# Projection weights: halves split for the first token half kept in DRAM and fetched for the second; gate differences on VectorE

## The chip, the cores and the metric

The kernel runs on one core of a Trainium2 chip. The metric is device time in microseconds, from the launch of the program to its end. The engines are named as in the profile: PE is TensorE's matmul, PEld its weight load, DVE is VectorE, ACT ScalarE, POOL GpSimd, and SP SyncE, which here only issues DMAs. A name such as SPq or POOLq is the engine's instruction queue.

## The reference

One layer over 1024 tokens of 1024 channels, all in float32: a norm with a shift and a scale that depend on the conditioning vector `c`, a wide input projection, two mixers (a pooling mixer and a gated linear attention), an output projection with a gated residual, then a second norm and a gated MLP with a causal convolution.

```python
mod = c_act @ ada_w[l] + ada_b[l]
sh1, sc1, g1, sh2, sc2, g2 = jnp.split(mod, 6, axis=-1)
h = modulate(rmsnorm(x), sh1, sc1)
u, q, k, v, r, z = jnp.split(h @ w_in[l], IN_SPLITS, axis=-1)
y_pool = pool_mixer(u, w_pool[l], pool_scale[l])
y_gla = gla_mixer(q, k, v, r, z, w_gate2[l], b_gate[l], gla_norm[l])
y = jnp.concatenate([y_pool, y_gla], axis=-1) @ w_out[l]
x = x + g1[:, None, :] * y
h = modulate(rmsnorm(x), sh2, sc2)
x = x + g2[:, None, :] * conv_ffn(h, w_up[l], conv_w[l], conv_b[l], w_down[l])
...
return rmsnorm(x) * final_norm
```

In the attention, `b` is the running sum of log gates; a score of two tokens carries `exp` of a difference of two such sums.

## The kernel before

Channels lie on the 128 partitions, in 8 tiles; the 1024 tokens are two halves of 512. Every projection is computed for the first half and later again for the second, with the same weights, since only then are the second half's activations there.

**Split products.** A float32 product is made of three faster ones. A weight tile of 512 KB is loaded into one of four buffers (`raw`, from the pool `rawp`, L62), ACT casts it to its high part `wh` (L152), DVE subtracts that from it, which gives the low part `wl` (L153), and `mm3` (L113) multiplies high by high, high by low and low by high. Two buffers each hold `wh` and `wl`. The four raw buffers also serve the tiles `ada` of the conditioning product (L215 to L220: a load by SP, then a DVE product whose sum goes into `modv`), of which 20 come beside the projections r, u and out. `load_w` (L156) does load and split; it runs for each tile in each half.

**Jobs.** A job is one weight tile's work: `job_proj` (L612) 24 matmuls for one output tile of q, k, r or u, `jobs_v` (L636) and `jobs_out` (L667) two channel tiles of four outputs. `run_jobs` (L726) calls the load of the next job, runs the present one, then issues its `ada` products. In the second half the groups are k, z, q, k, v, q, then r0 to r3, then u0 to u3 (L761 to L763); `jobs_out(0)` follows, the output projection of the first half, then `jobs_out(1)`.

**Order.** PE's order is written out by the program: beside the jobs run generators (attention, pooling, norms) that are resumed when a counter of estimated PE time passes their due time. The order of the other engines is made by a scheduler from dependences; each engine then runs its own in order, SP's queue of DMA issues too.

**The attention** (`gla_pair`, L382) goes through seven levels for each of two pairs of heads in each half. For a level `gla_prep` (L337) takes a difference of gate sums `le` (POOL, L343 or L347), ACT takes exponentials (L351, L352), DVE makes `kl` (L356) and `lq` (L359), PE multiplies them (`sc`), and DVE copies the scores under a mask into `la` (L376). POOL makes `kd` (L403) and `le<-k,lb`, the product of q and k for the diagonal `dg` (L390).

**The ends.** The pooling mixer `pool_tail` (L511) copies u out of PSUM on ACT (`us`, L515), makes sums on DVE (L522), a difference (L532) and its split `dh`, `dl`, and a small product `po`, whose result goes to `yh` (ACT, L540) and `yl` (DVE, L541). The output projection adds to x on DVE and stores x1 to DRAM by SP (L695); the squares of x1 are added up on POOL (`nsa`, L234) for the second norm.

Of the kernel before, what the change touches and what calls it, by code (L numbers as in the profile page):

```python
# [28 lines left out]
P = 128  # L29
NK = 8  # L30
# [23 lines left out]
def trunk_kernel(ctx, tc, xT, cvec, adaT, vecs, w_start, w_z, w_qkru, w_v, w_g2, w_pool,  # L54
# [98 lines left out]
        dve.tensor_tensor(out=wl, in0=raw, in1=wh.bitcast(F32), op=ALU.subtract)  # L153
        return wh, wl

    def load_w(dram, shape=(P, NK, P)):  # L156
        raw = raw4(shape=shape)
        nc.sync.dma_start(out=raw, in_=dram)
        return split_w(raw, shape)

    def split_a(src, name):
        h, l = s2(F32R, name=name + "h"), s2(F32R, name=name + "l")
# [174 lines left out]
    def gla_prep(b, k, q2, h):  # L337
        nb = T // (2 * h)
        bb = blocks(b, h)
        e = tmp("le")  # L340
        eb = blocks(e, h)
        if h == 1:
            pool_e.tensor_tensor(out=eb[:, :, 1], in0=bb[:, :, 1], in1=bb[:, :, 0],  # L343
                                 op=ALU.subtract)
            kl = k
        else:
            pool_e.tensor_tensor(out=e.rearrange("p (n h) -> p n h", n=nb),  # L347
                                 in0=b.rearrange("p (n h) -> p n h", n=nb),
                                 in1=bb[:, :, 0, h - 1:h].broadcast_to([P, nb, 2 * h]),
                                 op=ALU.subtract)  # L350
            act.activation(out=eb[:, :, 0], in_=eb[:, :, 0], func=AF.Exp, scale=-1.0 / 16)  # L351
        act.activation(out=eb[:, :, 1], in_=eb[:, :, 1], func=AF.Exp, scale=1.0 / 16)  # L352
        if h > 1:
            kl = klb[mark.setdefault("kl", 0)]
            mark["kl"] ^= 1
            dve.tensor_tensor(out=blocks(kl, h)[:, :, 0], in0=blocks(k, h)[:, :, 0],  # L356
                              in1=eb[:, :, 0], op=ALU.mult)
        ql = tmp("lq", shape=(P, 2, T // 2))
        dve.tensor_tensor(  # L359
            out=ql.rearrange("p e (n h) -> p e n h", h=h),  # L360
            in0=q2.rearrange("p e (n two h) -> p e n two h", two=2, h=h)[:, :, :, 1],
            in1=eb[:, :, 1].unsqueeze(1).broadcast_to([P, 2, nb, h]), op=ALU.mult)
        return kl, ql
# [18 lines left out]
    def gla_pair(hf, ct):  # L382
# [17 lines left out]
        for i, h in enumerate(LEVELS):  # L400
            nxt = gla_prep(b, k, q2, LEVELS[i + 1]) if i + 1 < len(LEVELS) else None
            if i == 0:
                pool_e.tensor_tensor(out=chunks(kd), in0=chunks(b),  # L403
                                     in1=chunks(b)[:, :, P - 1:P].broadcast_to([P, 4, P]),
                                     op=ALU.subtract)
                act.activation(out=kd, in_=kd, func=AF.Exp, scale=-1.0 / 16)
                dve.tensor_tensor(out=kd, in0=kd, in1=k, op=ALU.mult)
            gla_scores(av, *pre, h)
            if i == 3:
                ktp = stile("ktp", (P, 4, P))  # L410
                for c in range(4):
# [12 lines left out]
            if i == 6:
                for hd in range(2):
                    dve.tensor_tensor(out=q2[:, hd], in0=q2[:, hd], in1=eq, op=ALU.mult)
            yield LEVEL_STEP[hf]
# [181 lines left out]
        if t is not None:  # L609
            mod_tile(t, True)  # L610

    def job_proj(dram, hf, then, last=False):  # L612
        def run(w):
            wh, wl = w
            pp = ptile()
            for k in range(NK):
                until(lambda: hs[hf][k] is not None)
                mm3(pp, wh[:, k], wl[:, k], *hs[hf][k], k == 0, k == NK - 1)
                if last:
                    nacc["gone"] = k + 1  # L620
                if k < NK - 1:
                    tick()
            then(pp)
        return (lambda: load_w(dram)), run

    def job_z(hf):
        def run(_):
# [8 lines left out]
    def jobs_v(hf):  # L636
        pv = []

        def mk(kp):
            def run(w):  # L640
                wh, wl = w
                if kp == 0:
                    pv.extend(ptile() for _ in range(4))
                for j in range(2):
                    k = 2 * kp + j
                    h, l = hs[hf][k]
                    for c in range(4):
                        cs = slice(c * P, c * P + P)
                        mm(pv[c], h[:, cs], wh[:, j], k == 0, False)
                        mm(pv[c], l[:, cs], wh[:, j], False, False)  # L650
                        mm(pv[c], h[:, cs], wl[:, j], False, k == NK - 1)
                        tick()
                if kp == 3:
                    for c in range(4):
                        vt[hf * 4 + c] = s2(name="v")
                        act.copy(out=vt[hf * 4 + c], in_=pv[c])
            return (lambda: load_w(w_v[kp], (P, 2, T))), run
        return [mk(kp) for kp in range(4)]

    def job_u(hf, gi):  # L660
        return job_proj(w_qkru[8 + gi], hf, lambda pp: spawn(pool_tail(hf, gi, pp)),
                        hf == 0 and gi == 3)

    def job_r(hf, n):
        return job_proj(w_qkru[4 + n], hf, lambda pp: put_r(pp, hf, n))

    def jobs_out(hf):  # L667
        po = []

        def mk(i):  # L670
            d0, kp = 4 * (i // 4), i % 4

            def run(w):
# [7 lines left out]
                for j in range(2):  # L681
                    k = 2 * kp + j
                    until(lambda: ys[hf][k] is not None)
                    for n in range(4):
# [2 lines left out]
                        if k == NK - 1:  # L687
                            evac(d0 + n, po[n])
                        tick()
            return (lambda: load_w(w_out[i], (P, 2, T))), run  # L690

        def evac(d, pp):
            dve.scalar_tensor_tensor(out=x1[hf][d], in0=pp, scalar=modv[:, 16 + d:17 + d],  # L693
                                     in1=x1[hf][d], op0=ALU.mult, op1=ALU.add)
            nc.sync.dma_start(out=x1d[hf][d], in_=x1[hf][d])  # L695
            own = s2 if hf else None
            if d == 0:
                nacc[hf] = s2(name="nsa") if hf else tmp("nsa")
# [24 lines left out]
            hs[0][k] = mod_split(x1[0][k], 24, k)  # L723
            yield 2.0

    def run_jobs(jobs, mods_each=0):  # L726
        loaded = jobs[0][0]()
        for i, (_, run) in enumerate(jobs):
            nxt = jobs[i + 1][0]() if i + 1 < len(jobs) else None
            run(loaded)  # L730
            loaded = nxt
            for _ in range(mods_each):
                mod_next()
            tick()
# [6 lines left out]
    run_jobs([job_u(0, n) for n in range(4)])  # L741

    def job_q(ct):
        load, run = job_proj(w_qkru[ct], 1, lambda pp: put_q(pp, 1, ct))

        def go(w):
            until(lambda: ys[0][4 + 2 * ct] is not None)
# [1 line left out]
        return load, go  # L749

    def job_k(ct):
        return job_proj(w_qkru[2 + ct], 1, lambda pp: put_k(pp, 1, ct))

    named = {"z": job_z(1)}
    for ct in range(2):
# [4 lines left out]
        named[f"v{n}"] = j  # L760
    for names, mods_each in (("k0 z q0 k1 v0 v1 v2 v3 q1", 0), ("r0 r1 r2 r3", 2),  # L761
                             ("u0 u1 u2 u3", 1)):
        run_jobs([named[i] for i in names.split()], mods_each)  # L763
    run_jobs(jobs_out(0), 2)
    spawn(norm2_first())
    late = jobs_out(1)
    run_jobs(late[:5], 1)
    until(lambda: hs[0][7] is not None)
    ph1.close()
    phr.close()  # L770
# [507 lines left out]
```

## Time and profile before

| | us |
|---|---|
| median of 3 runs | 1082.6 |
| range of the runs | 1080.9 to 1084.25 |
| profiled execution | 1082.63 |
| its span | 1080.9 |
| PE busy | 1021.6 |
| DVE busy | 856.0 |
| ACT busy | 546.2 |
| POOL busy | 200.1 |

The span is the time from the first to the last instruction of the profiled execution. In all, DMA moved 152.64 MB. By stage: up to about 54 us the first half's norm and its k, q and two r tiles; to 189 us the rest of the first half's projections and its attention; to 337 us the second half's projections with its attention, then the first half's output; to 400 us the second half's output; behind that the MLP, which the change does not touch.

In a row of the timeline stand start, duration, engine, line, operation, output and inputs; in brackets how long the engine was idle before it, and what ended that. In a row of the waits stand the total in microseconds, the number of waits and the longest.

### The profile page before, as it was taken

The numbers are of one execution on the slowest core, as the hardware profiler recorded it, in microseconds if no ns is written. First come the engines' busy times: TensorE is split into PE (matmuls) and PEld (weight loads), VectorE is DVE, ScalarE is ACT, GpSimd is POOL, SyncE is SP. The second block draws the span as 40 slices with busy tenths as digits, with TensorE's granted clock in tenths as the row PEclk, the third lists the DMA queues.
The fourth block names the chain that finished last, engine by engine and source line by source line (L and its number), as shares of the span: only waits on it lengthen the run. The fifth ranks groups of instructions, "written<-read, shape, count | busy, mean of one in ns | idle before, by whom it ended". The sixth has DMA issues, their size and how long they took to land.

```text
span 1080.9 us, 12664 instructions
## 1 busy us (share of the span) xinstructions
PE 1021.6 (95%) x4480; PEld 816.2 (76%) x4480; DVE 856.0 (79%) x1189; ACT 546.2 (51%) x881; POOL 200.1 (19%) x171
## 2 busy tenths in 40 slices
PE   6989999999898986899999999999999999999986
PEld 4668878887786764688888888888888888888875
DVE  7967999688897959997776777767767686988884
ACT  5475484534534435655554555545545544644542
POOL 3436203131132115011011010010110100200210
PEclk8999999999899998999999999999999999999998
DMA  8743331454577530232223223322233895323542
GB/s 311 256 137 106 98 112 64 148 184 136 166 262 253 202 129 20 78 117 98 88 89 117 88 98 108 108 107 98 106 127 111 294 328 193 98 98 98 187 154 78
DMA packets 60385, 152.64 MB, mean 141 GB/s; under 512 B 6593, under 2 KB 9761, under 8 KB 60322
## 3 DMA queue, kind: packets, MB, share of 16 engines
q1 hardware_dynamic: 53760, 132.43, 36.2%
q0 software_dynamic: 4928, 17.30, 4.1%
q10 hardware_dynamic: 1634, 2.10, 0.6%
q8 instruction: 35, 0.57, 0.2%
q14 instruction: 28, 0.23, 0.1%
HBM read 126.12 MB, written 25.69 MB: 140 GB/s over the span
## 4 chain that ended last, share of the span: by engine, by line
PE 74%; DVE 16%; DMA 3%; ACT 3%; issue 3%; POOL 1%; SPq 0%; POOLq 0%; ACTq 0%; DVEq 0%
PE dn L107 18%; PE upy L107 17%; PE pp L107 14%; PE upz L107 11%; PE upx L107 10%; DVE wl L153 2%; PE sc L107 1%; DVE ada L219 1%; DVE hl L275 1%; DMA ada<-in_adaT_dram 1%; PE ss L107 1%; DVE la L376 1%; DMA da<-in_w_down_dram 1%; DVE sl L887 1%; DVE x L267 1%
## 5 line engine op out<-in xcount | busy, mean ns | idle before, releaser
L107 PE MATMUL dn<-ws,xs 128*128 128x512 f32 (+1 forms) x936 | 212.9, 389 | 2.8 <-DVE xs L1087 2.8
L107 PEld LDWEIGHTS dn<-ws,xs 128*128 128x128 f32 x936 | 175.3, 189 | 40.0 <-issue 3.7
L107 PE MATMUL upy<-sh,xs 128*128 128x512 f32 x272 | 92.2, 400 | 6.1 <-ACT upy L937 6.1
L107 PE MATMUL upy<-sh,ws 128*128 128x512 f32 x256 | 85.7, 395 | 0.9 <-ACT upy L937 0.9
L975 POOL DMA_DIRECT2D gd<-y x22 | 12.0, 545 | 372.6 <-DVE y L974 372.6
L793 DVE TENSOR_TENSOR xs<-ua,xs 128x512 fp32r<-128x512 f32 x77 | 54.8, 711 | 31.4 <-ACT xs L792 31.4
L153 DVE TENSOR_TENSOR wl<-raw,wh 128x1024 fp32r<-128x1024 f32 (+1 forms) x50 | 63.5, 1270 | 17.2 <-ACT wh L152 17.0
L107 PE MATMUL pp<-hl,wh 128*128 128x512 f32 x176 | 70.9, 403 | 5.4 <-DVE hl L275 5.4
L107 PE MATMUL pp<-hh,wh 128*128 128x512 f32 x176 | 73.9, 420 | 1.0 <-ACT hh L274 1.0
L792 ACT CAST xs<-ua 128x512 fp32r<-128x512 f32 x77 | 47.9, 622 | 52.1 <-PE upy L107 21.4
L107 PE MATMUL pp<-hh,wl 128*128 128x512 f32 x176 | 70.8, 402 | 2.3 <-DVE wl L153 2.3
L793 DVE TENSOR_TENSOR ws<-ua,ws 128x512 fp32r<-128x512 f32 x77 | 54.2, 704 | 22.1 <-ACT ws L792 22.1
L792 ACT CAST ws<-ua 128x512 fp32r<-128x512 f32 x77 | 48.0, 623 | 42.1 <-PE upy L107 20.6
L792 ACT CAST ws<-da 128x512 fp32r<-128x512 f32 x58 | 36.1, 622 | 63.9 <-PE dn L107 47.7
L107 PEld LDWEIGHTS upy<-sh,xs 128*128 128x128 f32 x272 | 51.8, 190 | 19.5 <-ACT upy L937 6.8
L803 DVE TENSOR_TENSOR ua<-ua 128x512 f32<-128x512 f32 x88 | 62.7, 713 | 2.2
L107 PE MATMUL upz<-sh,ws 128*128 128x512 f32 x184 | 62.2, 397 | 1.7 <-ACT sh L886 1.7
L152 ACT CAST wh<-raw 128x1024 fp32r<-128x1024 f32 (+1 forms) x50 | 50.4, 1008 | 24.1 <-PE pp L107 7.8
L107 PE MATMUL pp<-yh,wh 128*128 128x512 f32 x128 | 55.5, 434 | 6.7 <-ACT us L515 3.5
L107 PE MATMUL upx<-hh,xs 128*128 128x512 f32 x176 | 59.1, 397 | 2.4 <-ACT sp L953 2.4
L107 PE MATMUL upx<-hh,ws 128*128 128x512 f32 x176 | 59.3, 398 | 0.2 <-DVE x L693 0.2
L347 POOL TENSOR_TENSOR le<-b 128x512 f32<-128x512 f32 x24 | 33.7, 1406 | 137.7 <-PE dg L107 52.4
(252 smaller groups left out, 2461.1 us busy)
## 6 DMA issues: line engine op xcount, KB each, us to landing
ua<-in_w_up_dram SPq DMA_DIRECT2D x46, 512.0 KB, 3.3
ada<-in_adaT_dram SPq DMA_DIRECT2D x32, 512.0 KB, 3.8
gd<-y POOLq DMA_DIRECT2D x22, 512.0 KB, 2.9
raw<-in_w_qkru_dram SPq DMA_DIRECT2D x18, 512.0 KB, 3.5
da<-gd SPq DMA_DIRECT2D x36, 256.0 KB, 2.8
da<-in_w_down_dram SPq DMA_DIRECT2D x36, 256.0 KB, 3.4
raw<-in_w_out_dram SPq DMA_DIRECT2D x16, 512.0 KB, 4.3
x<-in_xT_dram SPq DMA_DIRECT2D x24, 256.0 KB, 4.5
```

What stands on the lines that cost most here:

```text
L107: pe.matmul(out=out, lhsT=lhsT, rhs=rhs, start=start, stop=stop, skip_group_check=more)
L152: act.copy(out=wh, in_=raw)
L153: dve.tensor_tensor(out=wl, in0=raw, in1=wh.bitcast(F32), op=ALU.subtract)
L219: dve.scalar_tensor_tensor(out=a, in0=a, scalar=1.0, in1=cb, op0=ALU.mult, op1=ALU.mult, accum_out=acc)
L267: dve.scalar_tensor_tensor(out=t, in0=x, scalar=modv[:, sc_c + k:sc_c + k + 1], in1=r, op0=ALU.mult, op1=ALU.mult)
L275: mark["split"] = dve.scalar_tensor_tensor(out=l, in0=t, scalar=sh, in1=h.bitcast(F32), op0=ALU.add, op1=ALU.subtract)
L347: pool_e.tensor_tensor(out=e.rearrange("p (n h) -> p n h", n=nb), in0=b.rearrange("p (n h) -> p n h", n=nb), in1=bb[:, :, 0, h - 1:h].broa ...
L376: dve.copy_predicated(out=av.rearrange("p a (n two h) -> p a n two h", two=2, h=h)[:, :, :, 1], mask=cit[:, mi].rearrange("p (n h) -> p n ...
L792: act.copy(out=h, in_=src)
L793: dve.tensor_tensor(out=l, in0=src, in1=h.bitcast(F32), op=ALU.subtract)
L803: eng.tensor_tensor(out=out, in0=a, in1=b, op=ALU.subtract)
L975: nc.gpsimd.dma_start(out=gd[i], in_=ya)
```

## The change

Four things change.

- `load_w` has a key. With one, the first half stores `wh` and `wl` of the tile to DRAM by POOL's queue, and the second half fetches both by SP into two tiles that matmuls use as they are; cast and subtraction are left out there. Fetches go in turn into two raw buffers (then the tiles are called `kw`) and into a `wh` and a `wl` buffer. It holds for 18 tiles: r2, r3, u0 to u3, the four of v and the eight of the output.
- Loads are called two jobs ahead, not one, in the second half's groups and the first five output jobs of the second half.
- The differences of gate sums (28) and of `kd` (4) go from POOL to DVE.
- The stores of x1 (16 of 256 KB) go from SP's queue to POOL's.

```diff
-    def load_w(dram, shape=(P, NK, P)):
+    kept = {}
+    fetched = [0]
+
+    def load_w(dram, shape=(P, NK, P), key=None):
+        if key in kept:
+            fetched[0] += 1
+            if fetched[0] % 2:
+                tiles = [rawp.tile(list(shape), F32R, tag="raw", name="kw", bufs=4)
+                         for _ in range(2)]
+            else:
+                tiles = [wp.tile(list(shape), F32R, tag=tag, name=tag) for tag in ("wh", "wl")]
+            for t, d in zip(tiles, kept[key]):
+                nc.sync.dma_start(out=t.bitcast(F32), in_=d)
+            return tiles
         raw = raw4(shape=shape)
         nc.sync.dma_start(out=raw, in_=dram)
-        return split_w(raw, shape)
+        w = split_w(raw, shape)
+        if key is not None:
+            kept[key] = [tc.dram_tile(list(shape), F32, name=f"kept_{key[0]}{key[1]}_{n}")
+                         for n in range(2)]
+            for d, t in zip(kept[key], w):
+                nc.gpsimd.dma_start(out=d, in_=t.bitcast(F32))
+        return w
...
-            pool_e.tensor_tensor(out=e.rearrange("p (n h) -> p n h", n=nb),
+            dve.tensor_tensor(out=e.rearrange("p (n h) -> p n h", n=nb),
...
-                pool_e.tensor_tensor(out=chunks(kd), in0=chunks(b),
+                dve.tensor_tensor(out=chunks(kd), in0=chunks(b),
...
-        return (lambda: load_w(dram)), run
+        return (lambda: load_w(w_qkru[n], key=("in", n) if n > 5 else None)), run
...
-            return (lambda: load_w(w_v[kp], (P, 2, T))), run
+            return (lambda: load_w(w_v[kp], (P, 2, T), ("v", kp))), run
...
-            return (lambda: load_w(w_out[i], (P, 2, T))), run
+            return (lambda: load_w(w_out[i], (P, 2, T), ("out", i))), run
...
-            nc.sync.dma_start(out=x1d[hf][d], in_=x1[hf][d])
+            nc.gpsimd.dma_start(out=x1d[hf][d], in_=x1[hf][d])
...
-    def run_jobs(jobs, mods_each=0):
-        loaded = jobs[0][0]()
+    def run_jobs(jobs, mods_each=0, ahead=1):
+        loaded = []
         for i, (_, run) in enumerate(jobs):
-            nxt = jobs[i + 1][0]() if i + 1 < len(jobs) else None
-            run(loaded)
-            loaded = nxt
+            while len(loaded) < min(i + 1 + ahead, len(jobs)):
+                loaded.append(jobs[len(loaded)][0]())
+            run(loaded[i])
...
-        run_jobs([named[i] for i in names.split()], mods_each)
+        run_jobs([named[i] for i in names.split()], mods_each, 2)
...
-    run_jobs(late[:5], 1)
+    run_jobs(late[:5], 1, 2)
```

The lines of the changed kernel are 19 higher behind `load_w` (L347 is L366, L343 L362, L403 L422, L390 L409, L219 L238, L376 L395).

How it moves instructions shows at three places. The first is the end of the first attention pair of the second half on DVE, beside u0. Before:

```order
L426 TENSOR_TENSOR lb<-lb,lm 128x512 x2
L219 SCALAR_TENSOR_TENSOR ada,macc<-ada,cb 128x1024
L153 TENSOR_TENSOR wl<-raw,wh 128x1024
L376 COPY_PREDICATED la<-cit,sc 128x256x2
L469 SCALAR_TENSOR_TENSOR st_155<-st_155,lm,sp 64x128 x4
```

In the changed kernel, at the same place:

```order
L445 TENSOR_TENSOR lb<-lb,lm 128x512 x2
L395 COPY_PREDICATED la<-cit,sc 128x256x2
L378 TENSOR_TENSOR lq<-lb,le 128x512
L488 SCALAR_TENSOR_TENSOR st_155<-st_155,lm,sp 64x128 x4
L366 TENSOR_TENSOR le<-b 128x512
L375 TENSOR_TENSOR kl_158<-k,le 128x8x32
```

The split and the `ada` product ahead of the masked copy `la` are gone, and the difference `le` of a later level stands directly ahead of the `kl` of that level.

The second is u2's part of the pooling mixer on DVE: its additions (L522 before, L541 after), the difference behind them (L532, L551) and the split `dl`. Before:

```order
L522 TENSOR_TENSOR us<-us 128x527
L153 TENSOR_TENSOR wl<-raw,wh 128x1024
L522 TENSOR_TENSOR us<-us 128x525
L225 SCALAR_TENSOR_TENSOR modv<-macc,vec 128x1
L522 TENSOR_TENSOR us<-us 128x521
L219 SCALAR_TENSOR_TENSOR ada,macc<-ada,cb 128x1024
```

In the changed kernel:

```order
L541 TENSOR_TENSOR us<-us 128x527
L541 TENSOR_TENSOR us<-us 128x525
L541 TENSOR_TENSOR us<-us 128x521
L551 SCALAR_TENSOR_TENSOR us<-us 128x512
L533 COPY us<-uh 128x16
L238 SCALAR_TENSOR_TENSOR ada,macc<-ada,cb 128x1024
L183 TENSOR_TENSOR dl<-us,dh 128x512
```

The three additions and the difference now follow one another; the `ada` product has moved behind them and the split is not there.

The third is SP's queue for the second half's output tiles 4 to 7 (`kept_out_0` and `kept_out_1` are the kept high and low part of a tile; the number is that of the tile in DRAM, and in the order of the tiles 2686 and 2687 are tile 4, 2769 and 2770 tile 5, 2832 and 2833 tile 6, 2906 and 2907 tile 7). Before:

```order
L158 DMA raw<-in_w_out_dram 128x1024
L680 DMA x_3107<-in_xT_dram 128x512
L680 DMA x_3109<-in_xT_dram 128x512
L680 DMA x_3111<-in_xT_dram 128x512
L680 DMA x_3113<-in_xT_dram 128x512
L158 DMA raw<-in_w_out_dram 128x1024 x2
```

In the changed kernel:

```order
L168 DMA wl<-kept_out_1_2907 128x1024
L819 DMA ua<-in_w_up_dram 128x1024
L699 DMA x_3354<-in_xT_dram 128x512
L699 DMA x_3356<-in_xT_dram 128x512
L168 DMA wh<-kept_out_0_2769 128x1024
L168 DMA kw<-kept_out_0_2832 128x1024
L168 DMA kw<-kept_out_1_2833 128x1024
L699 DMA x_3358<-in_xT_dram 128x512
```

The high part of tile 5 (2769) is issued behind the low part of tile 7, a load for the MLP (`ua`) and two x loads; before, a raw tile was one load.

More of the change, by code (lines that the diff above doesn't have):

```diff
@@ L342, in gla_prep @@
         if h == 1:
-            pool_e.tensor_tensor(out=eb[:, :, 1], in0=bb[:, :, 1], in1=bb[:, :, 0],
-                                 op=ALU.subtract)
+            dve.tensor_tensor(out=eb[:, :, 1], in0=bb[:, :, 1], in1=bb[:, :, 0],
+                              op=ALU.subtract)
             kl = k
         else:
[L347 to L350, printed above, removed]
+            dve.tensor_tensor(out=e.rearrange("p (n h) -> p n h", n=nb),
+                              in0=b.rearrange("p (n h) -> p n h", n=nb),
+                              in1=bb[:, :, 0, h - 1:h].broadcast_to([P, nb, 2 * h]),
+                              op=ALU.subtract)
             act.activation(out=eb[:, :, 0], in_=eb[:, :, 0], func=AF.Exp, scale=-1.0 / 16)
@@ L402, in gla_pair @@
             if i == 0:
-                pool_e.tensor_tensor(out=chunks(kd), in0=chunks(b),
-                                     in1=chunks(b)[:, :, P - 1:P].broadcast_to([P, 4, P]),
-                                     op=ALU.subtract)
+                dve.tensor_tensor(out=chunks(kd), in0=chunks(b),
+                                  in1=chunks(b)[:, :, P - 1:P].broadcast_to([P, 4, P]),
+                                  op=ALU.subtract)
                 act.activation(out=kd, in_=kd, func=AF.Exp, scale=-1.0 / 16)
@@ L610, in mod_next, with job_proj @@
             mod_tile(t, True)
-    def job_proj(dram, hf, then, last=False):
+    def job_proj(n, hf, then, last=False):
         def run(w):
@@ L656, in run @@
                         act.copy(out=vt[hf * 4 + c], in_=pv[c])
-            return (lambda: load_w(w_v[kp], (P, 2, T))), run
+            return (lambda: load_w(w_v[kp], (P, 2, T), ("v", kp))), run
         return [mk(kp) for kp in range(4)]
     def job_u(hf, gi):
-        return job_proj(w_qkru[8 + gi], hf, lambda pp: spawn(pool_tail(hf, gi, pp)),
+        return job_proj(8 + gi, hf, lambda pp: spawn(pool_tail(hf, gi, pp)),
                         hf == 0 and gi == 3)
     def job_r(hf, n):
-        return job_proj(w_qkru[4 + n], hf, lambda pp: put_r(pp, hf, n))
+        return job_proj(4 + n, hf, lambda pp: put_r(pp, hf, n))
     def jobs_out(hf):
@@ L743, in job_q @@
     def job_q(ct):
-        load, run = job_proj(w_qkru[ct], 1, lambda pp: put_q(pp, 1, ct))
+        load, run = job_proj(ct, 1, lambda pp: put_q(pp, 1, ct))
         def go(w):
@@ L751, in job_k @@
     def job_k(ct):
-        return job_proj(w_qkru[2 + ct], 1, lambda pp: put_k(pp, 1, ct))
+        return job_proj(2 + ct, 1, lambda pp: put_k(pp, 1, ct))
     named = {"z": job_z(1)}
```

## Prediction

> **What bounds the kernel now.** I read the page first, then a table of windows by stage, then the waits of TensorE, then the timeline at each of them.
>
> ```profile
> span 1080.9 us, 12664 instructions
> ```
>
> ```profile
> 54.00:189.00 135.00, 129.78 (x623) 104.59 (x623) 115.49 (x171) 83.48 (x144) 43.44 (x36) 0.99 0.31 104
> 189.00:337.00 148.00, 141.48 (x683) 115.68 (x682) 123.42 (x205) 64.17 (x108) 32.50 (x21) 0.98 0.57 187
> 337.00:400.00 63.00, 55.37 (x214) 39.92 (x213) 44.93 (x58) 27.29 (x41) 13.26 (x9) 0.97 0.55 188
> ```
>
> In the table each row gives the window, its length, then the busy time of PE, PEld, DVE, ACT and POOL, the granted clock, the DMA share and GB/s. The change touches 54 to 400 us only. There PE is busy 326.6 of 346 us: 19.4 us of idle time is nearly all that it can win. So the question is which of those microseconds disappear, and what new ones come. The waits of PE between 54 and 400 us (total, times, longest):
>
> ```profile
> PE pp L107 <- DVE wl L153: 3.9, 5, 1.4
> PE pp L107 <- ACT us L515: 3.5, 1, 3.5
> PE pp L107 <- ACT wh L152: 2.8, 3, 1.0
> PE ss L107 <- POOL nsa L234: 2.6, 1, 2.6
> ...
> PE op L107 <- DVE la L376: 1.1, 1, 1.1
> PE sp L107 <- DVE la L376: 1.1, 1, 1.1
> ```
>
> Splits (`wh`, `wl`) end 6.7 us of idle time, the evacuation `us` 3.5 us, the masked copies `la` 2.2 us. A stall costs more than its idle time, as the timeline of PE shows at the late output products:
>
> ```profile
> 381.64 0.39 PE L107 MATMUL pp<-yh,wl 128*128 128x512 f32 x1
> 383.02 0.50 PE L107 MATMUL pp<-yh,wh 128*128 128x512 f32 x1 [0.99 <-ACT wh L152]
> 383.36 0.40 PE L107 MATMUL pp<-yl,wh 128*128 128x512 f32 x1
> 384.27 0.50 PE L107 MATMUL pp<-yh,wl 128*128 128x512 f32 x1 [0.52 <-DVE wl L153]
> 384.61 0.39 PE L107 MATMUL pp<-yh,wh 128*128 128x512 f32 x1
> ...
> 389.28 0.40 PE L107 MATMUL pp<-yh,wl 128*128 128x512 f32 x1
> ```
>
> Undisturbed matmuls start 0.233 us apart (4.67 us from 384.61 to 389.28, 20 intervals). From 381.64 to 383.02 are 1.38 us, 1.15 too many, and the matmul after the stall takes 0.34 to the next one, 0.11 too many. So a stall costs its idle time plus 0.27 us.
>
> **What the change removes.** First, three stalls between 237 and 253 us: the two `la` rows above and this one, in the matmuls of u0 and of the attention beside them.
>
> ```profile
> 237.77 0.50 PE L107 MATMUL pp<-hh,wl 128*128 128x512 f32 x1 [0.82 <-DVE wl L153]
> ```
>
> Before, DVE runs an `ada` product and a split directly ahead of each late `la`; the order of the change has no split left there, since u0 to u3 come from DRAM ready split. One `wl` costs 1.28 us:
>
> ```profile
> L153 DVE TENSOR_TENSOR wl<-raw,wh 128x1024 fp32r<-128x1024 f32 x42 | 53.7, 1278 | 17.2 <-ACT wh L152 17.0
> ```
>
> That is more than each of the three waits. They go: 0.82 + 1.1 + 1.1 + 3 x 0.27 = **3.8 us**.
>
> Second, the longest stall. The timeline of ACT, then that of PE:
>
> ```profile
> 275.12 0.62 ACT L163 CAST dh<-us 128x512 fp32r<-128x512 f32 x1 [3.49 <-DVE us L532]
> ...
> 277.05 0.69 ACT L540 ACTIVATE yh<-po,vec 128x512 fp32r<-128x512 f32 x1
> 277.63 0.58 ACT L515 COPY us<-pp 128x512 f32<-128x512 f32 x1
> ```
>
> ```profile
> 274.35 0.40 PE L107 MATMUL pp<-yh,wl 128*128 128x512 f32 x1
> 278.26 0.79 PE L107 MATMUL pp<-yh,wh 128*128 128x512 f32 x1 [3.51 <-ACT us L515]
> ...
> 284.52 0.72 PE L107 MATMUL dg<-hsel,le 128*128 128x2 f32 x6
> ```
>
> ```profile
> 278.00:282.00 4.00, 3.74 (x9) 2.96 (x10) 3.88 (x6) 3.98 (x7) 0.00 (x0) 0.50 0.38 128
> ```
>
> The first output product needs the PSUM tile that `us` of u3 frees; `us` stands on ACT behind `dh` of u2, which waited for DVE. After the stall the granted clock is 0.50 for some 4 us. From 274.35 to 284.52 are 10.17 us for 16 intervals (15 matmuls lie between), which take 16 x 0.233 = 3.7 us undisturbed: **6.4 us**, stall and slow clock together. PE needs that tile at 274.35 + 0.23 = 274.58, and `us` ends at 278.21: 3.6 us are wanted. In the order of the change neither the split nor the `ada` that stood among u2's additions on DVE is there any more (2 x 1.28), nor u3's split among u1's steps ahead (1.28), so `dh` can come 3.8 us sooner, and ACT's order keeps `dh`, `yh`, table load and `us` close together. I count all 6.4; the margin is 0.2 us, and what an `ada` or a raw output tile lands later than that comes back as a wait here (0 to 3.7).
>
> Third, output tiles 5, 6 and 7 of the second half: six stalls, `wh` 2.8 plus the three smaller `wl` waits (0.52 in the row above; 0.59 and 0.53 in its neighbours, the rest of the 3.9 being 0.82 and 1.4), so 4.4 + 6 x 0.27 = **6.1 us**. Here a cast, a subtract and the matmuls run in series since only one `wh` buffer is left for them. Fetched pairs skip both steps.
>
> Sum of the gains: 3.8 + 6.4 + 6.1 = 16.3 us.
>
> **What it adds.** (a) 32 differences go from POOL to DVE. Their price on POOL, the price of such an operation on DVE, and what POOL does to DVE beside it:
>
> ```profile
> L347 POOL TENSOR_TENSOR le<-b 128x512 f32<-128x512 f32 x24 | 33.7, 1406 | 137.7 <-PE dg L107 52.4 <-DVE lq L359 45.1 <-DVE b L326 15.7
> ```
>
> ```profile
> L803 DVE TENSOR_TENSOR ua<-ua 128x512 f32<-128x512 f32 x88 | 62.7, 713 | 2.2
> ```
>
> ```profile
> 161.08 0.42 DVE L356 TENSOR_TENSOR kl<-k,le 128x256 f32<-128x256 f32 x1
> ...
> 163.91 1.26 DVE L356 TENSOR_TENSOR kl<-k,le 128x256 f32<-128x256 f32 x1
> ```
>
> ```profile
> 162.26 2.62 POOL L347 TENSOR_TENSOR le<-b 128x512 f32<-128x512 f32 x2 [11.58 <-ACT nsq L320]
> ```
>
> DVE gains 32 x 0.7 = 22 us and loses 18 `wl` x 1.28 = 23 us, but not at the same places: the first half has 16 more differences and every split still. The same `kl` takes 0.42 us alone and 1.26 beside POOL's difference, so each move also returns up to 0.84 us. The Trainium skill ("SBUF — State Buffer", "Who interferes with whom") has a VectorE instruction with two SBUF inputs contend with a GpSimd one that reads SBUF; the two `kl` rows agree. By it POOL's remaining reads (qk, `nsa`) still stretch DVE, and where the differences did, the sum has 0.6 us less. The fullest stretch of the first half, and of the output product:
>
> ```profile
> 150.00:189.00 39.00, 39.00 (x201) 31.58 (x200) 36.84 (x57) 23.39 (x43) 10.86 (x9) 1.00 0.21 68
> ```
>
> ```profile
> 297.00:324.00 27.00, 27.00 (x141) 22.79 (x140) 26.34 (x46) 9.44 (x16) 10.11 (x5) 1.00 0.79 266
> ```
>
> From 150 to 189 us eight more at 0.6 to 0.7 are some 5 us, of which about 2.2 return as stretch and 2.2 are idle: I charge **0.6 us** to the first half (bounds -1 to +3). In the output stretch DVE has 0.7 us free: 5 us more against about 2.5 returned; I charge **2.0 us**, with DMA below (0 to 6).
>
> (b) 36 stores of 512 KB on POOL, and x1's 16 stores there instead of SP's queue. Issues and the sums of squares on POOL:
>
> ```profile
> L975 POOL DMA_DIRECT2D gd<-y x22 | 12.0, 545 | 372.6 <-DVE y L974 372.6
> ```
>
> ```profile
> L234 POOL TENSOR_TENSOR nsa<-nsa,nsq 128x512 f32<-128x512 f32 x19 | 31.6, 1664 | 76.8 <-ACT nsq L230 76.1
> ```
>
> Six stores now stand on POOL ahead of the qk product for the first attention pair, in place of two differences and the `kd` one of about 1.3: 6 x 0.55 = 3.3 against 4, about even. The stall of 2.6 us on `nsa` (norm 2 of the first half) is a chain on POOL; three x1 stores between its additions add 3 x 0.55 = **1.7 us** (0.55 to 2.2; cover only if POOL ran ahead, which the stall denies).
>
> (c) Fetched pairs. 18 x 512 KB more are read, and a pair is in the place of the raw tile. A load's landing, from the page:
>
> ```profile
> ada<-in_adaT_dram SPq DMA_DIRECT2D x32, 512.0 KB, 3.8
> ...
> raw<-in_w_out_dram SPq DMA_DIRECT2D x16, 512.0 KB, 4.3
> ```
>
> A pair's second tile is not in the trace; between 4.3 (in parallel) and 8.6 us (in series), I take 5, nearest the one row, since all engines serve each transfer. Output jobs last 24 x 0.233 = 5.6 us. For output 5 SP's list has the `wh` half behind the release by job 3, a `ua` and two x loads: late by 1.3 us (0 to 2.5). A pair that takes over the raw buffers of the pair before is issued when that product ends, and has the job between, 5.6 us or more, to land: on time with 5, 3 us late with 8.6, most closely for u0. I charge **1.8 us** for both (0 to 5). A pair also holds two of the four raw buffers until its product ends, so `ada` loads pass through two; with 3.8 + 1.3 us a round that is enough.
>
> Costs: 0.6 + 2.0 + 1.7 + 1.8 = 6.1. Net 16.3 - 6.1 = 10.2 us. The profiled run took 1082.63 us (span 1080.9), as the median of the runs, 1082.6: **1072 us**.
>
> **Rivals.** (1) DMA is full during the first output product:
>
> ```profile
> 10.00:20.00 10.00, 5.47 (x15) 3.32 (x15) 8.89 (x11) 6.40 (x10) 4.54 (x2) 0.66 1.03 418
> ...
> 310.00:320.00 10.00, 10.00 (x53) 8.48 (x52) 10.00 (x14) 1.51 (x2) 5.32 (x2) 1.00 0.93 297
> ```
>
> In the output product's row (297 to 324) DMA moves 266 GB/s. Stores of 8 x 1.05 MB in 65 us add 129, doubled fetches some 20: 415 GB/s. At 418, the highest seen, it just fits; at 297/0.93 = 319, what the second row scales to, those 27 us last 27 x (415/319 - 1) = 8 us longer. Less the 2.0 charged above: 1072 + 6 = **1078**. By the Trainium skill ("DMA: Bandwidth & Descriptors", "Where 436 GB/s comes from") HBM gives about 358 GB/s to a core, which speaks against the change and would be 27 x (415/358 - 1) = 4 us; the row of 418 exceeds that figure.
>
> (2) No net change: pairs come late everywhere, a new wait for the old one. From a pair's landing above the 5.6 us of a job on, each microsecond above costs as much on each of about 10 pairs that are issued at a product's end: 1 us gives 1072 + 10 = **1082**.
>
> (3) Slower: DVE sets the pace of the attention. It works in order, and between a difference and the `kl` that needs it ACT takes two exponentials:
>
> ```profile
> 91.16 0.42 ACT L351 ACTIVATE le<-le 128x256 f32<-128x256 f32 x1 [2.47 <-POOL le L347]
> 91.48 0.40 ACT L352 ACTIVATE le<-le 128x256 f32<-128x256 f32 x1
> ```
>
> If nothing fills those 0.82 us, a pair costs 8 x 0.7 + 7 x 0.82 = 11.3 us more; for the two pairs beside a full DVE 22.6, less the idle 2.2 + 0.7 there: 19.7. With the 2.6 already charged taken off: **1089**. Against it: the order mostly has one or two instructions of 0.6 to 0.7 in between, and POOL's stretching ends. It decides when DVE's lead over PE is less than those 10 us a pair.
>
> That the change does nothing is excluded: 18 `wl` are gone in the order.
>
> **How the numbers follow.** Forecast 0.55, DMA 0.18, no net 0.12, slower 0.15. The forecast's own bounds: all costs at their lowest, 1082.6 - 16.3 - 1 + 0.55 = 1066; at their highest (3 + 6 + 2.2 + 5 = 16.2, without the 3.7 at `us`) 1082.5. Lower still only by stalls that I left standing (2.6 at `nsa`, 1.4 at an earlier `wl`): 1063. The upper end at 1086 leaves most of (3) out, some 0.13, and 0.05 lie below. A measurement tells 0.3% (3.2 us) from no change, so faster is below 1079.4: 0.55 x 0.95 + 0.18 x 0.8 + a little of (2), 0.71; same 0.14; slower 0.15.
>
> **What would show it.** Right: no waits on `wl` or `wh` between 230 and 260 and after 370; no slow clock near 280; fewer than 1 us of waits on a fetched pair each; DVE's `kl` at 0.42. Wrong: waits for `kw` or `wh` DMAs on PE, PE waiting for `kl` or `lq` near 80 to 190, DVE idle behind `ada`, `nsa` well above 4.3.

## The result and the profile after

The changed kernel takes 1092.68 us (median of 4 runs, 1091.65 to 1094.59) against 1083.21 us for the kernel before (1080.9 to 1084.25): a ratio of 1.010, 95% interval 1.008 to 1.0119. It is 9.5 us slower. The forecast was 1072, with a range of 1063 to 1086; the measured time lies above the range, and the change went the other way.

The page of the profiled execution of the changed kernel, its first line and two rows of its DMA part:

```profile
span 1091.9 us, 12731 instructions
...
q0 software_dynamic: 11392, 40.38, 9.4%
...
HBM read 135.56 MB, written 44.56 MB: 165 GB/s over the span
```

Written are 18.9 MB more (25.69 before), read 9.4 more (126.12). To see where the time goes, I compared when the same instruction of PE starts in both traces. A plus is late:

| instruction of PE | before | after | late by |
|---|---|---|---|
| first gates `gp` | 67.65 | 70.94 | +3.3 |
| first transposes `ktp` | 100.02 | 107.02 | +7.0 |
| third diagonal `dg` (second half) | 206.04 | 212.11 | +6.1 |
| a small product `po` of the pooling mixer, ahead of the output | 270.29 | 273.06 | +2.8 |
| fourth `dg` | 284.52 | 281.17 | -3.3 |
| fourth `ktp`, in the first output product | 305.78 | 303.00 | -2.8 |
| attention output `op` | 326.98 | 330.94 | +4.0 |
| last head norm `on` | 349.31 | 352.56 | +3.2 |
| first product of the MLP, `upx` | 397.44 | 401.61 | +4.2 |
| sum of squares `ss` of the second half | 404.48 | 413.63 | +9.1 |
| end of the span | 1080.9 | 1091.9 | +11.0 |

So 3.3 us are won from 206 to 270, another 6.1 us to 284; lost are 7.0 us in the head (up to the first `ktp`), 6.8 in the first output product, and 5.9 from 349 to 404. The 1.9 us behind 404 are made up of two things. A `DRAIN` on POOL's queue, behind the last product of the kernel, takes longer. Before, then after (the third duration is the longest of three, in ns):

```profile
L1273 POOLq DRAIN  x3: 40/102/4432, 1075.6 to 1080.6; - x3
```

```profile
L1292 POOLq DRAIN  x3: 40/93/8679, 1082.5 to 1091.7; - x3
```

That is 4.25 us more, with 52 DMAs more on POOL's queue (36 stores of weights, 16 of x1): 0.082 us for each. From `ss` to the start of that drain the changed kernel is 2.3 us shorter (668.8 us, 671.2 before).

Each column of the table is one trace. e12 below has the same edits as the changed kernel up to the first fetch, and its first `ktp` is 1.1 us earlier; so a difference of about a microsecond between two traces says little.

The waits of PE in the stretches of the table, from its timeline before, then in the changed kernel:

```profile
67.65 0.50 PE L107 MATMUL gp<-le,g2w 96*128 96x512 f32 x1 [0.84 <-ACT le L310]
...
401.59 0.50 PE L107 MATMUL upx<-hh,xs 128*128 128x512 f32 x1 [1.09 <-ACT sp L953]
```

```profile
70.94 0.79 PE L107 MATMUL gp<-le,g2w 96*128 96x512 f32 x1 [4.24 <-ACT le L329]
82.58 1.87 PE L107 MATMUL dg<-hsel,le 128*128 128x2 f32 x8 [2.50 <-POOL le L409]
...
243.84 0.50 PE L107 MATMUL pp<-hh,kw 128*128 128x512 f32 x1 [0.57 <-DMA kw<-kept_in]
...
306.37 0.47 PE L107 MATMUL pp<-yh,wh 128*128 128x512 f32 x1 [1.36 <-ACT le L371]
309.12 0.50 PE L107 MATMUL pp<-yh,wh 128*128 128x512 f32 x1 [1.12 <-DVE x L712]
...
317.74 1.83 PE L107 MATMUL sc<-lq,kl 128*128 128x128 f32 x8 [1.13 <-DVE lq L378]
...
382.58 0.59 PE L107 MATMUL pp<-yh,wh 128*128 128x512 f32 x1 [3.36 <-DMA wh<-kept_out]
...
408.39 0.79 PE L107 MATMUL upx<-hh,xs 128*128 128x512 f32 x1 [3.75 <-ACT sp L972]
```

Gone are the waits at 237 to 253 and the stall of 3.51 us near 278, with its slow clock; each new wait of over 3 us brings a slow clock of its own (0.50 from 70 to 74 us, 0.59 from 383 to 387, 0.50 from 408 to 412). What stands behind the first of the new waits shows on ACT:

```profile
69.66 0.63 ACT L249 ACTIVATE nsa<-nt 128x512 f32<-128x512 f32 x1 [3.81 <-DMA nt<-in_xT_dram]
70.31 0.57 ACT L329 CAST le<-pz 32x512 fp32r<-32x512 f32 x1
```

The square for the second half's norm waits 3.8 us for its first x tile (`nt`), and the cast that PE's gate product needs is queued behind it on ACT. In the kernel before the square had no wait:

```profile
65.86 0.62 ACT L230 ACTIVATE nsa<-nt 128x512 f32<-128x512 f32 x1
```

DMA in that time, in the table of windows of the changed kernel (share and GB/s are the last two columns):

```profile
66.00:68.00 2.00, 0.70 (x3) 0.21 (x2) 0.85 (x2) 0.00 (x0) 0.53 (x1) 1.00 1.05 415
68.00:70.00 2.00, 0.00 (x0) 0.00 (x0) 0.00 (x0) 0.34 (x1) 0.00 (x0) 0.70 1.03 412
```

All DMA engines are busy there; in the kernel before, the row of 66 to 68 us has a share of 0.32 and 82 GB/s. Busy is not the same as fast: from 62 to 65 us, while this load was under way, the changed kernel's share was 0.92 at only 213 GB/s, for which no run here gives a reason. The eight `nt` tiles, from issue to landing, before and then after:

```profile
DMA to landing us min/median/max: 2.7/3.0/3.9
```

```profile
DMA to landing us min/median/max: 2.6/5.0/8.3
```

The first output product reads the same way: ACT waits 6.6 us for a raw output tile (issued at 291.88, so 10.7 us from its issue to the cast), while the share of DMA is 0.99.

```profile
302.58 1.05 ACT L152 CAST wh<-raw 128x1024 fp32r<-128x1024 f32 x1 [6.57 <-DMA raw<-in_w_out_dram]
```

```profile
290.00:303.00 13.00, 13.00 (x69) 10.94 (x69) 9.89 (x20) 4.03 (x8) 1.06 (x2) 1.00 0.99 365
```

```profile
raw<-in_w_out_dram SPq DMA_DIRECT2D x8, 512.0 KB, 6.4
```

The last row, from the page's DMA issues, has 6.4 us for the raw output tiles, 4.3 before.

### The profile page after: what moved, and what is told of

It reads as the page before. It is cut to its first block, busy times and chain, and to the rows that moved or that the text cites. A ratio compares the mean times of both kernels' runs of the same rounds, so it can differ in the third digit from the quotient of the medians.

```text
span 1091.9 us, 12731 instructions
## 1 busy us (share of the span) xinstructions
PE 1026.2 (94%) x4480; PEld 820.7 (75%) x4480; DVE 842.5 (77%) x1203; ACT 530.8 (49%) x863; POOL 179.7 (16%) x191
## 4 chain that ended last, share of the span: by engine, by line
PE 76%; DVE 11%; DMA 6%; issue 3%; ACT 2%; POOL 1%; SPq 0%; POOLq 0%; ACTq 0%; DVEq 0%
PE dn L107 17%; PE upy L107 17%; PE pp L107 15%; PE upz L107 11%; PE upx L107 10%; DMA ada<-in_adaT_dram 2%; DMA raw<-in_w_out_dram 2%; DVE wl L153 1%; PE sc L107 1%; PE ss L107 1%; DVE ada L238 1%; DVE hl L294 1%; PE op L107 1%; DMA nt<-in_xT_dram 1%; DVE sl L906 1%
## 5 line engine op out<-in xcount | busy, mean ns | idle before, releaser
L994 POOL DMA_DIRECT2D gd<-y x22 | 11.9, 539 | 372.7 <-DVE y L993 372.7
L107 PE MATMUL pp<-hl,wh 128*128 128x512 f32 x152 | 62.7, 413 | 5.1 <-DVE hl L294 5.1
L107 PE MATMUL pp<-hh,wh 128*128 128x512 f32 x152 | 65.4, 430 | 1.3 <-ACT hh L293 1.3
L107 PE MATMUL pp<-hh,wl 128*128 128x512 f32 x152 | 62.0, 408 | 0.0
L941 DVE SCALAR_TENSOR_TENSOR y<-ca,vec,y 128x1023 f32<-128x1023 f32 (+1 forms) x44 | 56.4, 1281 | 3.7 <-ACT y L938 3.0
L153 DVE TENSOR_TENSOR wl<-raw,wh 128x1024 fp32r<-128x1024 f32 (+1 forms) x32 | 39.5, 1234 | 25.0 <-ACT wh L152 23.9
L941 DVE SCALAR_TENSOR_TENSOR y<-cb,vec,y 128x1023 f32<-128x1023 f32 (+1 forms) x44 | 56.3, 1280 | 2.0 <-ACT y L938 2.0
L107 PEld LDWEIGHTS upy<-sh,ws 128*128 128x128 f32 x256 | 48.0, 187 | 13.1 <-ACT upy L956 1.4
```

What stands on the lines that cost most here:

```text
L107: pe.matmul(out=out, lhsT=lhsT, rhs=rhs, start=start, stop=stop, skip_group_check=more)
L941: dve.scalar_tensor_tensor(out=y[:, sh:], in0=c[:, :S - sh], scalar=cw[j], in1=y[:, sh:], op0=ALU.mult, op1=ALU.add)
L994: nc.gpsimd.dma_start(out=gd[i], in_=ya)
```

## The experiments

The theories: **A**, the stores fill the DMA engines, and what is loaded beside them lands late; **B**, the gate differences on VectorE cost the time; **C**, fetched tiles hold buffers that later work wants. Each run's ratio is to the kernel before, run on the same chip.

### e1: the stores left out

```diff
-            kept[key] = [tc.dram_tile(list(shape), F32, name=f"kept_{key[0]}{key[1]}_{n}")
-                         for n in range(2)]
-            for d, t in zip(kept[key], w):
-                nc.gpsimd.dma_start(out=d, in_=t.bitcast(F32))
+            kind = shape[1]
+            if key in (("in", 8), ("v", 3)):
+                for d, t in zip(alike[kind], w):
+                    nc.gpsimd.dma_start(out=d, in_=t.bitcast(F32))
+            kept[key] = alike[kind]
```

`alike` holds two tiles in DRAM, a high and a low part, for each of the two tile shapes.

> The changed kernel, but only the halves of two weight tiles (u0 and v3) are stored, 4 stores instead of 36; every fetch of the second half reads one of those two pairs, as many bytes as before, so the products of the other tiles use a wrong weight (work is left out: 32 stores of 512 KB). Theory A, the stores fill the DMA engines and what else is loaded beside them lands late (the norm's nt tile at 61 to 70 us, the raw output tiles at 297 to 331): both losses of about 7 us go, so 1092.7 - 14 = about 1079 us; nt lands in about 3 us and TensorE's wait of 4.2 us ahead of gp is under 1 us. Theory B, the gate differences on VectorE cost the time: nothing changes, 1090 to 1095. Theory C, the fetched tiles hold buffers that later loads want: the loss behind 350 us stays, also under A.

Measured: 1080.8 us, ratio 0.9972 (0.9959 to 0.9985), 11.9 us below the changed kernel; 2.6 of that is POOL's drain, 6.07 us here. `gp` starts at 68.19 behind a wait of 0.83; from the fourth `ktp` to `op` 1.4 us are lost, not 6.8. So A holds for both places. Of the 7.0 us in the head it explains about half: at the first `ktp` e1 is still 3.7 us late, which e2 takes up. C holds as well: from 349 to 404 us e1 loses 6.6 us, no less than the changed kernel.

```profile
371.56 0.50 PE L107 MATMUL pp<-yh,wh 128*128 128x512 f32 x1 [3.88 <-DMA wh<-kept]
...
397.47 0.80 PE L107 MATMUL upx<-hh,xs 128*128 128x512 f32 x1 [3.75 <-ACT sp L975]
```

These are PE's two long waits there, as in the changed kernel. DMA is full at the first of them. What is stored there, up to 371 us, is x1; from then on POOL's queue moves nothing, and loads alone fill DMA:

```profile
368.00:372.00 4.00, 0.44 (x2) 0.40 (x3) 1.29 (x2) 1.14 (x2) 0.00 (x0) 1.00 1.04 421
371.00:375.00 4.00, 3.44 (x10) 2.72 (x11) 0.00 (x0) 0.00 (x0) 0.00 (x0) 0.69 1.04 419
```

### e2: nothing kept

```diff
-        return (lambda: load_w(w_qkru[n], key=("in", n) if n > 5 else None)), run
+        return (lambda: load_w(w_qkru[n], key=None)), run
...
-            return (lambda: load_w(w_v[kp], (P, 2, T), ("v", kp))), run
+            return (lambda: load_w(w_v[kp], (P, 2, T))), run
...
-            return (lambda: load_w(w_out[i], (P, 2, T), ("out", i))), run
+            return (lambda: load_w(w_out[i], (P, 2, T))), run
```

> The changed kernel without keeping: no store and no fetch, each weight tile is loaded raw and split in both halves as in the kernel before; loads two jobs ahead, gate differences on VectorE and x1 stores on GpSimd's queue stay. Theory A (stores) and theory C (fetched tiles' buffers): within 5 us of the kernel before, 1079 to 1088. Theory B (gate differences on VectorE cost): 1090 or more.

Measured: 1085.4 us, ratio 1.0018 (1.0007 to 1.0029). B is not the main cause, but it is not nothing: the other parts of the change alone lose 2 us. Of these 1.3 are POOL's drain (5.74 us, with x1's 16 stores there). In its trace the first `ktp` is 3.4 us late without any store of weights. DVE, then POOL, in e2:

```profile
74.30 1.25 DVE L366 TENSOR_TENSOR le<-b 128x512 f32<-128x512 f32 x1
75.47 1.75 DVE L422 TENSOR_TENSOR lm<-b 128x512 f32<-128x512 f32 x1
77.14 1.75 DVE L341 TENSOR_TENSOR lq<-lq,nsq 128x512 f32<-128x512 f32 x1
```

```profile
73.70 1.30 POOL L253 TENSOR_TENSOR nsa<-nsa,nsq 128x512 f32<-128x512 f32 x1 [16.64 <-issue]
74.96 3.38 POOL L409 TENSOR_TENSOR le<-k,lb 64x512 f32<-64x512 f32 x2
```

The differences now stand on DVE beside POOL's product of q and k, and take 1.25 and 1.75 us, not 0.7; the product takes 3.38, 2.67 before, and stands behind a sum for the norm. PE waits 3.54 us for it, 2.46 before.

### e3: gate differences back on GpSimd

```diff
-            dve.tensor_tensor(out=e.rearrange("p (n h) -> p n h", n=nb),
+            pool_e.tensor_tensor(out=e.rearrange("p (n h) -> p n h", n=nb),
...
-                dve.tensor_tensor(out=chunks(kd), in0=chunks(b),
+                pool_e.tensor_tensor(out=chunks(kd), in0=chunks(b),
```

> The changed kernel with the 32 gate differences back on GpSimd, all else as changed. Theory A: the losses at 61 to 110 us and at 300 to 331 us stay, and the masked copies wait beside GpSimd again: 1091 to 1098. Theory B (the differences on VectorE cost): 1080 to 1086.

Measured: 1093.7 us, ratio 1.0098 (1.007 to 1.0125). B falls as the main cause. In its trace PE waits 3.57 us for a masked copy at 326.84. The first `ktp` is 5.8 us late, though the differences are on GpSimd; so with the stores there the two losses of the head do not simply add up.

### e4 and e5: only u kept, and the first half's differences back

e4:

```diff
-        return (lambda: load_w(w_qkru[n], key=("in", n) if n > 5 else None)), run
+        return (lambda: load_w(w_qkru[n], key=("in", n) if n > 7 else None)), run
...
-            return (lambda: load_w(w_v[kp], (P, 2, T), ("v", kp))), run
+            return (lambda: load_w(w_v[kp], (P, 2, T))), run
...
-            return (lambda: load_w(w_out[i], (P, 2, T), ("out", i))), run
+            return (lambda: load_w(w_out[i], (P, 2, T))), run
```

e5 has this besides:

```diff
+        eng = dve if hf else pool_e
+        pre = gla_prep(b, k, q2, LEVELS[0], eng)
```

with `eng` in the place of `dve` for the differences.

> The changed kernel, but only u0 to u3 are kept (8 stores, 4 fetched pairs); r, v and the output tiles are loaded raw and split in both halves. Theory A: no store lies in the head or beside the first output product, so those losses go, while the gains of 2.7 us at 237 to 256 us and of about 6 us at the stall near 278 us stay; the serial stalls of the output tiles 5 to 7 are back: 1083 - 9 = about 1074 us. Theory B: 1085 to 1092. Theory C: the loss behind 350 us goes here, which A alone does not tell apart; with e1 it does.

> As e4 (only u0 to u3 kept), and the gate differences of the first half's attention back on GpSimd, those of the second half on VectorE. In e4 the first diagonal product dg starts 1.7 us later than in the kernel before and the first transposes 3.9 us later, and another 0.7 us goes at the second half's gates (gp). Theory D, in the first half the differences on VectorE run beside GpSimd's products and sums and both are stretched (1.25 and 1.75 us for one difference): the 3.9 and the 0.7 go, 1080.9 - 4.6 = about 1076.5 us, and dg starts within 0.5 us of 77.1. Rival, they come from the scheduler's other order through two jobs ahead or the x1 stores: 1080 to 1082.

Measured: e4 1080.9 us, ratio 0.9978 (0.9962 to 0.9995); e5 1081.0, ratio 0.9985 (0.9969 to 1.0001). Both forecasts missed; e5's time is what its rival had, but its first `dg` is where theory D had it. The stalls from 237 to 284 us do go in both traces (the fourth `dg` is 7.6 us early in e4, 9.1 in e5), and in e5's trace the first `dg` starts at 77.27 and the first `ktp` is 1.5 us late, not 3.9. But of e4's lead of 7.6 us, 5.8 are lost by 397 us, and POOL's drain (6.39 us, with 24 DMAs more than before) takes 2.0 in both. e5's runs were no faster than e4's, though in its trace `ss` came 4.0 us earlier; 2.2 of these are gone at the start of the drain, and where is open.

### e6 and e8: r2 and r3 not kept; the output not kept

```diff
-        return (lambda: load_w(w_qkru[n], key=("in", n) if n > 5 else None)), run
+        return (lambda: load_w(w_qkru[n], key=("in", n) if n > 7 else None)), run
```

```diff
-            return (lambda: load_w(w_out[i], (P, 2, T), ("out", i))), run
+            return (lambda: load_w(w_out[i], (P, 2, T))), run
```

> The changed kernel, but r2 and r3 are not kept (loaded raw and split in both halves), so that no store lies ahead of 77 us. Theory A, the stores of r2 and r3 delay the first nt tile of the second half's norm, and through the square on ScalarE the gate product gp: gp is back at 67.6 to 68.3 us (70.9 in the changed kernel) and the time falls by 3 to 5.5 us, 1087 to 1090. Rival, nt is late for another reason (the issue order on SyncE's queue): gp stays near 70.9, 1092 to 1094.

> The changed kernel, but the eight output tiles are not kept (raw load and split in both halves); r2, r3, u and v are. Theory A and C: the head keeps its loss of 6 to 7 us, the loss of about 7 us from 303 to 331 us goes since no store lies there, and TensorE's wait on ACT sp in the MLP's first product (3.75 us) falls to about 1.2 as in e2, while the serial stalls of tiles 5 to 7 are back: e4 plus 3 us from the head, about 1084. If the 303 to 331 loss stayed, it would not be the output tiles' stores.

Measured: e6 1086.6 us, ratio 1.0041 (1.0025 to 1.0056); `gp` starts at 68.19. Its row:

```profile
68.19 0.50 PE L107 MATMUL gp<-le,g2w 96*128 96x512 f32 x1 [0.84 <-ACT le L329]
```

So the stores of r2 and r3, 2 MB, make the wait of 4.2 us at `gp`. The time fell by 6.1 us, somewhat more than the forecast's 3 to 5.5. e8: 1086.6 us, ratio 1.0032 (1.0012 to 1.0052). Its head loses 7.3 us to the first `ktp` as before, and from the fourth `ktp` to `op` it loses 1.4, as e1 and e4: 5.4 of the 6.8 us are the output tiles' stores. The wait on `sp` is 1.22.

### e7: late jobs and x1 stores as before

```diff
-    run_jobs(late[:5], 1, 2)
+    run_jobs(late[:5], 1)
...
-            nc.gpsimd.dma_start(out=x1d[hf][d], in_=x1[hf][d])
+            nc.sync.dma_start(out=x1d[hf][d], in_=x1[hf][d])
```

> As e5, and the first five late output jobs load one job ahead again and x1 is stored by SyncE's queue again. Of the change there remain u0 to u3 kept, two jobs ahead in the groups of the second half, and the second half's gate differences on VectorE. Between 349 us and the MLP's first product e4 lost 3.0 us against the kernel before. Theory E, that loss is from the two jobs ahead there or the x1 stores: 2 to 3 us below e5, 1073 to 1075. Rival, it is the gain from an earlier start lost at a load that comes no earlier: as e5, within 1.5 us.

Measured: 1079.0 us, ratio 0.9966 (0.9954 to 0.9979). Theory E falls: from 349 to 397 us its trace loses 2.5 us, much as e4 (3.1) and e5 (2.7). It is 2 us below e5 in the runs, between the forecast and its rival. Of that, 1.3 are POOL's drain, 5.09 us against 6.40, since x1's stores are off its queue; the rest is open.

### e9, e10 and e11: late output tiles kept too; u alone

e9 is e7 with the first of these lines, e10 with the second; e11 is e7 with the third and with all differences on `pool_e`.

```diff
+            return (lambda: load_w(w_out[i], (P, 2, T), ("out", i) if i > 4 else None)), run
...
+            return (lambda: load_w(w_out[i], (P, 2, T), ("out", i) if i in (5, 6) else None)), run
...
+        run_jobs([named[i] for i in names.split()], mods_each)
```

> As e7, and output tiles 5, 6 and 7 are kept too (5 and 7 fetched into raw buffers, 6 into wh and wl). Theory F, the fetched pairs in raw buffers keep the MLP's loads (ua) out: the serial stalls of about 2 us a tile go (6 us), but TensorE's wait on ACT sp in the MLP's first product is 3 us or more again, as in the changed kernel: 1076 to 1080. Rival, that wait comes from the DMA engines being full there: it stays near 1.1 and the time is 1073 to 1075.

> As e9, but tile 7 is loaded raw and split, so that no raw buffer is held by a pair when the MLP's loads come. Theory F: two of the three serial stalls go (4 us), the wait on ACT sp stays near 1.1 to 1.3: 1074 to 1076. Rival (full DMA engines, since 4 more stores lie at 305 to 325 us): 1078 to 1082, with TensorE's waits in the first output product.

> Only u0 to u3 kept; all gate differences on GpSimd, loads one job ahead everywhere and x1 stored by SyncE, as in the kernel before. Theory G, the splits of u that stood ahead of the masked copies and among the pooling mixer's additions made the stalls at 237 to 253 and 274 to 284 us: both go without the gate differences moved, 1078 to 1080 as e7. Rival, the differences on VectorE are needed for it: 1081 to 1083.

Measured: e9 **1073.9 us**, ratio 0.9914 (0.9899 to 0.9929): below both kernels. e10 1076.0, ratio 0.9942 (0.9925 to 0.9958). e11 1079.1, ratio 0.9958 (0.994 to 0.9975), as theory G had it. Theory F falls as I had put it: raw buffers held by pairs don't delay the MLP. (e9's time is in its rival's range; e10's is at the end of theory F's, which it met although the theory is wrong: PE's wait on `sp` is 1.08 there, and tile 7 keeps its two stalls.) In e9:

```profile
374.81 0.50 PE L107 MATMUL pp<-yh,wh 128*128 128x512 f32 x1 [0.41 <-DMA wh<-kept_out]
...
390.26 0.51 PE L107 MATMUL upx<-hh,xs 128*128 128x512 f32 x1 [0.68 <-ACT sp L973]
```

One wait of 0.41 is left of the six serial stalls, and the MLP waits 0.68. (At 333.91 the second half's output waits 3.54 us for the evacuation before it, 1.37 in e7: the six stores of the kept output tiles are not free either, it seems, but no run separates them.) e11 shows that the splits of u made the stalls up to 270 us (as early as e7 there), but in the stall near 278 a part stays, so that one needs the differences or the loads moved as well:

```profile
274.58 0.50 PE L107 MATMUL pp<-yh,wh 128*128 128x512 f32 x1 [2.38 <-ACT us L534]
```

### e12: the turn of the fetches flipped

In e9 tiles 5 and 7 came into raw buffers; in the changed kernel they come into `wh` and `wl`. One number turns that round in the full change:

```diff
-    fetched = [0]
+    fetched = [1]
```

> The changed kernel with the turn of the fetches flipped: the pairs that went to the raw buffers go to wh and wl and the other way round, so that output tiles 5 and 7 are fetched into raw buffers and 6 into wh and wl, as in e9. Theory H, the loss behind 349 us (5.9 us against the kernel before, 3.4 us idle for the high part of tile 5, 3.75 us in the MLP's first product) comes from tiles 5 and 7 having to pass through the one wh buffer that the MLP's first weight leaves, not from the stores: both waits go, the MLP's first product waits about 0.7 us, and the time is 1083 to 1087. Rival, it comes from the eight output pairs as such (bytes that land there): 1090 to 1094, with the waits on the fetches at another tile.

Measured: 1083.6 us, ratio 1.0007 (0.9985 to 1.0028), some 9 us below the changed kernel with the same stores and fetches. From `on` at 349 to `ss` at 404 it wins 4.5 us against the kernel before, where the changed kernel loses 5.9. Theory H holds. At 404 its trace is 5.9 us ahead of the kernel before; 4.25 of these go to POOL's drain, which is as long as the changed kernel's (8.68 us), and 1.7 are lost ahead of it. PE's waits between 349 and 404, e12:

```profile
375.07 0.72 PE L107 MATMUL pp<-yh,kw 128*128 128x512 f32 x2 [0.89 <-DMA kw<-kept_out]
...
395.65 0.50 PE L107 MATMUL upx<-hh,xs 128*128 128x512 f32 x1 [0.68 <-ACT sp L972]
```

What tile 7 does in the changed kernel is seen on ACT: the cast for the MLP's next weight, which takes a buffer of `wh`, starts only when PE is done with tile 7.

```profile
400.99 0.62 ACT L811 CAST ws<-ua 128x512 fp32r<-128x512 f32 x1 [0.17 <-PE pp L107]
```

In e12 the same cast starts at 390.92, ahead of the MLP's first product at 391.94.

## Why the prediction was wrong

Set beside the table, the sum is 21 us off: 5.5 up to 206 us (0.6 forecast, 6.1 measured), 5.3 from 284 to 331 (2.0, 7.3), 10.2 from 349 to 404 (a gain of 4.3, a loss of 5.9) and 1.9 behind; the rest is +0.8 and -2.4. So two steps failed, the fetches (c) at the late output tiles and the stores (b).

**The gains, first and second term: right.** For 237 to 253 us the text had 3.8; from 206 to 270 us the trace has 3.3. For the stall near 278 and its slow clock it had 6.4; the trace has 6.1.

**Third term, 6.1 us at tiles 5 to 7, and step (c): the larger failure. Right that the stalls go, wrong that this is a gain.** The text priced the late fetch of tile 5 at 1.3 us (0 to 2.5). It took 3.36 us idle and a slow clock, and the text had no term at all for tile 7's hold on the buffers that the MLP's first weights want (3.75 us). With the other turn of fetches (e12) the stretch wins 4.5 us, against 5.9 lost: 10.4 us of the traces hang on which pair of buffers a tile comes into. SP's order, shown ahead of the prediction, had this in it: tile 5's `wh` issued behind a later tile's `wl`.

**Step (b), the stores: the other step that failed.** It counted what stores cost to issue on POOL's queue, 0.55 us each, and found the head "about even". What they cost is DMA time. Beside the four stores of r2 and r3, issued from 60 to 67 us, a 256 KB load takes up to 8.3 us, DMA is full from 66 to 72 us, and since ACT works in order the load is on PE's path. DMA was examined only in the first output product; in the head the table had one average, a share of 0.31 from 54 to 189 us. e6 takes away the stores of r2 and r3, and with them the wait. The step also had no term for the end of the program, where the 52 DMAs more on POOL's queue make its drain 4.25 us longer: that the change "touches 54 to 400 us only" was wrong.

**Step (a), 0.6 us in the first half (bounds -1 to +3): too low, but inside its bounds.** Without any store of weights it is 2.5 us up to 206 us (e2). By e4 against e5, which differ in nothing else, the first half's differences make 1.6 us there, little more than two traces differ by; what makes the rest is not shown. The text counted what DVE gets back when POOL does less; not that POOL's product of q and k and its sums stay, and now stretch the differences themselves. The Trainium skill ("SBUF — State Buffer", "Who interferes with whom") has a VectorE instruction with two SBUF inputs contend with a GpSimd one that reads SBUF. The rows of e2 agree, and both sides are longer there: up to 1.75 us for a difference and 3.38 for the product.

**The output product, 2.0 us, and rival 1.** The rival named what happened there and priced it at 8 us in place of the 2.0; the trace has 6.8 from the fourth `ktp` to `op`, and e1 and e8 show that 5.4 of it are the stores. It had 0.18. It was taken as an alternative for one place, while the same cause worked in two. That its 8 us came close is partly luck: it took 319 GB/s for full DMA, and from 297 to 324 us the changed kernel moved 383 at a share of 1.00, with which its formula gives 2.3 us. The loss came by single loads that landed late, not by the average. Nor is there one rate of full DMA here: 415 and 412 in the windows of the head, 365 at a share of 0.99 from 290 to 303 us. By the Trainium skill ("DMA: Bandwidth & Descriptors", "Where 436 GB/s comes from") HBM gives a core about 358. These windows are above that, and the measurement decides.

**`nsa`, 1.7 us:** the wait fell from 2.62 to 1.86 us, and 0.8 us are won there. Rival 2 (late pairs everywhere) is wrong: for r, u and v one wait of 0.57. Rival 3 (DVE sets the pace) is wrong as the cause: e3. That its 1089 is nearest to the measured time is luck.

**Behind 404 us.** POOL's drain accounts for 4.25 us of loss there. It follows the number of DMAs on POOL's queue in every trace: 14 more than before make it 1.15 us longer (e9), 24 make 1.96 (e4), 52 make 4.25 (the changed kernel, e3 and e12). Why it does is not shown. The MLP between `ss` and the drain, which the change doesn't touch, lasts 668.8 to 672.8 us across the profiles of these runs; those differences stay open.

## What to carry to other kernels

A store that nobody waits for still has a price: the DMA time of every load beside it and, on POOL's queue here, 0.08 us at the end of the program. Before moving work to DRAM, put the bytes into the windows where they fall, at both ends, and ask which load there stands ahead of which instruction on an in-order engine. Keep only what a wait was seen for: here seven tiles of eighteen, with the differences moved for the second half alone, won 0.9% (e9); the full change loses 1%. And where a transfer goes straight into a working buffer, look who wants that buffer next.

## What the runs showed of the hardware

DMA moved 412 to 415 GB/s with loads and stores mixed (66 to 70 us) and 419 with loads alone (e1), but a share of 0.99 was 365 GB/s from 290 to 303 us, and one of 0.92 was 213 from 62 to 65 us. A 256 KB load among six transfers of 512 KB, issued from 60 to 66.5 us, took 8.3 us; the median before was 3.0. POOL's drain at the end of the program took 4.43 us in the kernel before, and 0.082 us more for each DMA that the runs put on its queue besides, up to 52. A long wait of PE costs twice: behind the 4.24 us at `gp` the granted clock was 0.50 from 70 to 74 us, and 3.3 us of delay at that `gp` were 5.4 at the next.
